# The output projection of two recurrences computed by itself and added to x in DRAM

## The chip, the cores and the metric

One core of a Trainium2 chip. The metric is the device time of one execution in microseconds: 3542.82 us, the median of three runs (3540.81 to 3544.31). The engines are named as in the profile: PE is TensorE, DVE is VectorE, ACT is ScalarE, POOL is GpSimd, and SP issues DMAs.

## The reference, cut to what matters

Two blocks of a network run one after the other on x (512 tokens by 1024 channels, float32). The first has two layers, each of them

```python
x = x + 0.5 * swiglu(rms_norm(x, ffn_norm[l, 0]), ...)
p = rms_norm(x, mix_norm[l]) @ w_in[l]
pa, pb, pc = split_cols(p, GROUP_SPLITS)
ya = dsa_attention(pa, ...)           # 512 channels
yb, v_first = rwkv7_time_mix(pb, ...) # 256 channels
yc = gated_deltanet(pc, ...)          # 256 channels
x = x + jnp.concatenate([ya, yb, yc], axis=-1) @ w_out[l]
x = x + 0.5 * swiglu(rms_norm(x, ffn_norm[l, 1]), ...)
```

The change touches the line with `w_out` in both layers. The 1024 input channels of that product are eight groups of 128: groups 0 to 3 come from the attention, 4 and 5 from the first recurrence (RWKV), 6 and 7 from the second (gated delta net). The second block is not touched.

## The kernel before

Everything is kept with channels on the 128 partitions and the 512 tokens along the free dimension, so x is eight tiles of 128x512. A float32 product is made of three matmuls (`mm3`): both operands are split into a high and a low part (`split`, `slab`), and high by high, high by low and low by high are accumulated in one PSUM bank. Weights come in slabs of 128x1024: a DMA issued by SP into one of three raw buffers, a cast on ACT and a subtraction on DVE into one of two pairs of high and low buffers.

The class `Mix` is one layer's middle part. It stores x to a DRAM tile `xd`, since the eight `x` buffers serve the attention meanwhile, computes the projections, two halves of each recurrence and the attention for four token tiles, and ends with the output projection by `down`.

The order of instructions on each engine isn't the order of the code. A planner sorts it when the kernel is built: among the instructions that can run, by its own estimate of times, the one with the smallest priority number comes first, and buffers and banks are handed out in that order. `stream(tag, level)` sets both the priority (a higher level is taken later) and the pool of buffers. The recurrences run at levels 0 and 1, the attention (`att`) at level 1, the weights and `down` at level 2, and the split of the recurrences' outputs into `yh` and `yl` at level 5. Once sorted, each engine runs its list strictly in order.

PSUM has eight banks in four pairs: `pj` (projections), `c` and `a` (the two halves of a recurrence) and `x` (the attention). For the last two token tiles the attention takes its transposed probabilities `pT` from the `pj` pair (`att(2, "x", "pj")` and `att(3, "x", "pj")`), four transposes to a bank, then a copy to SBUF by DVE or ACT in turn, and then the matmuls into `o`. In `att`, eight heads go in two groups of four; for tile 3 each group has four `pT` banks.

`down` works on half of the output channels at a time: four banks, one for each 128 channels, take all eight input groups, and then DVE adds each bank to x. For `Mix` the first half uses the pairs `c` and `a`, the second `pj` and `x`. Input groups are taken in the order 4, 5, 6, 7, 0, 1, 2, 3, two to a slab. So the first half's matmuls for the recurrences can run while the attention still works, and everything of the second half waits for `pj` and `x`. Before it x is loaded back from `xd` into eight fresh buffers. The following feed-forward part begins with the first four tiles of the new x.

Of the kernel before, what the change touches and what calls it, by code (L numbers as in the profile page):

```python
# [14 lines left out]
ALU = mybir.AluOpType  # L15
# [81 lines left out]
class Net:  # L97
# [3 lines left out]
    def __init__(self, ctx, tc, cst):  # L101
        self.ctx, self.tc, self.nc = ctx, tc, tc.nc
        nc = self.nc
        self.xp = ctx.enter_context(tc.tile_pool(name="xp", bufs=1))
        self.sm = ctx.enter_context(tc.tile_pool(name="sm", bufs=2))
        self.fp = ctx.enter_context(tc.tile_pool(name="fp", bufs=1))
        self.wraw = ctx.enter_context(tc.tile_pool(name="wraw", bufs=3))
        self.whi = ctx.enter_context(tc.tile_pool(name="whi", bufs=2))
        self.wlo = ctx.enter_context(tc.tile_pool(name="wlo", bufs=2))
        self.ps = ctx.enter_context(tc.tile_pool(name="ps", bufs=1, space=bass.MemoryType.PSUM))  # L110
        self.dr = ctx.enter_context(tc.tile_pool(name="dr", bufs=1, space=bass.MemoryType.DRAM))
        self.cst = self.xp.tile([128, _CN], F32, name="cst")
        self.reset = self.xp.tile([128, T], BF16, name="reset")
        nc.gpsimd.memset(self.reset, 1.0)
        nc.gpsimd.memset(self.reset[:, 0:T:64], 0.0)
        self.uid = 0
        self.tags = ["cag"[i % 3] for i in range(33)] + ["c", "a"] * 5 + ["g"]
        self.tag = "w"
        self.base = 0
        self.next = {}  # L120
# [207 lines left out]
class Mix:  # L328
# [3 lines left out]
    def __init__(self, net, l, x, par, w_in, lup, v_down, v_up, w_out, vfirst):  # L332
        self.n, self.tc, self.nc = net, net.tc, net.nc
        self.l, self.x, self.par, self.w_in, self.vfirst = l, x, par, w_in, vfirst
        nc, n = self.nc, net
        self.sm = net.sm
        (self.xh, self.xl, self.r), self.rc = net.split_x(x, self.p("mix_norm"))
        xd = n.dr.tile([128, KD, T], F32, name=f"xd{l}")
        for k in range(KD):
            nc.sync.dma_start(out=xd[:, k], in_=x[k])  # L340
        self.lp = net.xp.tile([128, 256], F32, tag="lp", name="lp")
        nc.scalar.dma_start(out=self.lp, in_=lup)
        if l:
            self.v_down, self.v_up = v_down, v_up
        self.kr = []
        self.y, self.yh, self.yl = [None] * 8, [None] * 8, [None] * 8
        chain = lambda tag="c", level=0: n.stream(tag, level)

        def go(part, tag="c", level=0):

            with n.stream(tag, level):
                next(part, None)

        r0, r1, g0, g1, at = self.rwkv(0), self.rwkv(1), self.gdn(0), self.gdn(1), self.att_in()
        self.misc()
        with chain("x", 1):
            self.index_in()
        with chain("c", 0):
            self.rwkv_in()
            self.kr.append(self.rwkv_kr(0))  # L360
        with chain("a", 0):
            self.kr.append(self.rwkv_kr(1))
        with chain("x", 1):
            for t in range(1, 4):
                self.index(t)
        go(r0, "c", 0)
        go(r1, "a", 0)
        go(at, "g", 1)
        with chain("c", 0):
            self.gdn_in()  # L370
        go(g0, "c", 0)
        go(r0, "c", 0)
        go(at, "g", 1)
        go(g1, "a", 0)
        go(r1, "a", 0)
        go(g0, "c", 1)
        go(g1, "a", 0)
        go(g0, "c", 0)
        with chain("g", 1):
            self.att(0, "x", "x")  # L380
            self.att(1, "x", "x")
        go(g1, "a", 0)
        with chain("g", 1):
            self.att(2, "x", "pj")
        with chain("g", 1):
            self.att(3, "x", "pj")
            self.att_out()
        with n.stream("c", 5):
            for i in (4, 5, 6, 7):
                self.yh[i], self.yl[i] = n.f("yh", F32R), n.f("yl", F32R)  # L390
                n.split(self.y[i], self.yh[i], self.yl[i])
        x[:] = [n.f("x", tag="x") for _ in range(KD)]
        with n.stream("w", 2):
            for k in range(KD):
                nc.sync.dma_start(out=x[k], in_=xd[:, k])
            net.down(x, self.yh, self.yl, w_out, [4, 5, 6, 7, 0, 1, 2, 3], 1.0,
                     (("c", "c", "a", "a"), ("pj", "pj", "x", "x")))

    def p(self, name, j=None):
        o, n = _PO[name]  # L400
# [1189 lines left out]
```

## Time and profile before

| | |
|---|---|
| median of three runs | 3542.82 us |
| the profiled execution's own time | 3542.9 us |
| its span | 3541.1 us |
| PE busy | 3414.4 us, 96% of the span |
| DVE busy | 2010.9 us, 57% |
| ACT busy | 1274.9 us, 36% |
| POOL busy | 84.7 us, 2% |
| mean granted PE clock | 0.965 |
| traffic with HBM | 100 GB/s over the span |

The span is what the profiler sees between the first and the last instruction; 1.8 us of the execution lie outside it. A share of busy time is a mean over very different stretches: the feed-forward parts have PE busy without a gap, the two `Mix` parts end in a stretch of small, dependent steps. Layer 0's output projection lies between 748 and 834 us of the span, layer 1's ends at 2023 us. In the timeline a line shows start, length, engine, line of the code, operation, output and inputs, and how many instructions are merged; a matmul's shown length is longer than the distance to the next one, because matmuls overlap.

### The profile page before, as it was taken

How to read it: one execution, taken by the hardware profiler on the slowest of the kernel's cores; microseconds unless marked ns; L12 is line 12 of the kernel's file. 1: busy time of each engine (PE TensorE's matmuls, PEld its weight loads, DVE VectorE, ACT ScalarE, POOL GpSimd, SP SyncE). 2: the span in 40 equal slices, each digit the busy share in tenths (PEclk: the TensorE clock that was granted, in tenths of full speed). 3: DMA queues.
4: the chain of work that ended last, by engine and by line, in shares of the span. 5: the costliest groups of instructions: out<-in, count | busy, mean ns of one | idle time of the engine just before them, and what ended most of it. 6: DMA issues, size and time to landing. Idle time of an engine off the chain costs nothing.

```text
span 3541.1 us, 44468 instructions
## 1 busy us (share of the span) xinstructions
PE 3414.4 (96%) x17314; PEld 2801.3 (79%) x17314; DVE 2010.9 (57%) x4364; ACT 1274.9 (36%) x2060; POOL 84.7 (2%) x168
## 2 busy tenths in 40 slices
PE   8999999889999999999998899999999999989999
PEld 7888778668888888887877688888777888778887
DVE  5555688765555555559978555535785332473332
ACT  4332544453332233335344433324563222232321
POOL 0000010000000000001100000000000000000000
PEclk9999999789999999999978999999999999989999
DMA  5346321103335434552210233432202333223332
GB/s 164 119 140 210 112 66 50 30 16 115 123 122 190 152 119 122 192 156 65 52 49 14 84 115 124 131 110 79 78 7 83 96 100 97 69 78 99 97 95 95
DMA packets 329955, 355.73 MB, mean 100 GB/s; under 512 B 41192, under 2 KB 249480, under 8 KB 329616
## 3 DMA queue, kind: packets, MB, share of 16 engines
q1 hardware_dynamic: 328576, 351.03, 32.5%
q8 instruction: 136, 2.23, 0.3%
q10 hardware_dynamic: 1168, 1.85, 0.2%
q14 instruction: 75, 0.61, 0.1%
HBM read 338.68 MB, written 14.16 MB: 100 GB/s over the span
## 4 chain that ended last, share of the span: by engine, by line
PE 89%; DVE 7%; ACT 2%; issue 1%; DMA 1%; POOL 0%; SPq 0%; DVEq 0%; ACTq 0%; POOLq 0%
PE pg L168 13%; PE pg L170 13%; PE pg L169 13%; PE pd L168 8%; PE pd L169 8%; PE pd L170 8%; PE pf L169 2%; PE pf L170 2%; PE pf L168 2%; PE lv L691 2%; PE G L904 1%; PE pt L430 1%; PE pt L431 1%; PE pt L429 1%; DVE wlo L162 1%
## 5 line engine op out<-in xcount | busy, mean ns | idle before, releaser
L162 DVE TENSOR_TENSOR wlo<-wraw,whi 128x1024 fp32r<-128x1024 f32 (+2 forms) x504 | 609.3, 1209 | 958.8 <-ACT whi L161 958.1
L161 ACT CAST whi<-wraw 128x1024 fp32r<-128x1024 f32 (+2 forms) x504 | 524.8, 1042 | 1283.6 <-PE pd L169 505.4
L168 PE MATMUL pg<-xh,whi 128*128 128x512 f32 x2112 | 825.5, 391 | 14.1 <-ACT whi L161 10.6
L170 PE MATMUL pg<-xh,wlo 128*128 128x512 f32 x2112 | 824.0, 390 | 0.0
L169 PE MATMUL pg<-xl,whi 128*128 128x512 f32 x2112 | 823.9, 390 | 0.0
L168 PEld LDWEIGHTS pg<-xh,whi 128*128 128x128 f32 x2112 | 398.1, 189 | 97.0 <-ACT whi L161 10.6
L169 PEld LDWEIGHTS pg<-xl,whi 128*128 128x128 f32 x2112 | 397.9, 188 | 83.1 <-DVE xl L273 0.6
L170 PEld LDWEIGHTS pg<-xh,wlo 128*128 128x128 f32 x2112 | 397.6, 188 | 83.5 <-DVE wlo L162 0.8
L168 PE MATMUL pd<-h,whi 128*128 128x512 f32 x1056 | 410.9, 389 | 0.0
L170 PE MATMUL pd<-h,wlo 128*128 128x512 f32 x1056 | 410.9, 389 | 0.0
L169 PE MATMUL pd<-h,whi 128*128 128x512 f32 x1056 | 410.8, 389 | 0.0
L1106 DVE CUSTOM_DVE_ANT_0 araw<-araw,act 128x512 f32<-128x512 f32 x224 | 148.9, 688 | 145.9 <-DMA araw<-in_ada_w_dram 140.6
L169 PEld LDWEIGHTS pd<-h,whi 128*128 128x128 f32 x1056 | 198.2, 188 | 41.3
L170 PEld LDWEIGHTS pd<-h,wlo 128*128 128x128 f32 x1056 | 198.2, 188 | 41.2
L168 PEld LDWEIGHTS pd<-h,whi 128*128 128x128 f32 x1056 | 198.2, 188 | 40.9
L168 PE MATMUL pf<-xh,whi 128*128 128x512 f32 (+4 forms) x424 | 167.0, 395 | 0.9 <-ACT xh L272 0.9
L169 PE MATMUL pf<-xl,whi 128*128 128x512 f32 (+4 forms) x424 | 167.3, 395 | 0.4 <-DVE xl L273 0.4
L170 PE MATMUL pf<-xh,wlo 128*128 128x512 f32 (+4 forms) x424 | 166.7, 393 | 0.0
L294 ACT ACTIVATE t<-t 128x512 f32<-128x512 f32 x88 | 55.6, 632 | 252.4 <-DVE t L293 250.6
L174 DVE TENSOR_TENSOR h<-t,h 128x512 fp32r<-128x512 f32 x132 | 90.8, 690 | 65.0 <-ACT h L173 64.7
L173 ACT CAST h<-t 128x512 fp32r<-128x512 f32 x132 | 81.8, 620 | 123.6 <-DVE t L296 76.7
L169 PEld LDWEIGHTS pf<-xl,whi 128*128 128x128 f32 (+2 forms) x424 | 79.1, 187 | 17.9 <-DVE xl L273 2.5
(494 smaller groups left out, 4692.8 us busy)
## 6 DMA issues: line engine op xcount, KB each, us to landing
wraw<-in_ffn_w_dram SPq DMA_DIRECT2D x132, 512.0 KB, 3.7
araw<-in_ada_w_dram SPq DMA_DIRECT2D x112, 512.0 KB, 3.5
wraw<-in_ffn_w_gate_dram SPq DMA_DIRECT2D x88, 512.0 KB, 3.8
wraw<-in_ffn_w_up_dram SPq DMA_DIRECT2D x88, 512.0 KB, 4.5
wraw<-in_ffn_w_down_dram SPq DMA_DIRECT2D x88, 512.0 KB, 3.6
wraw<-in_w_in_dram SPq DMA_DIRECT2D x69, 512.0 KB, 3.8
wraw<-in_w_out_dram SPq DMA_DIRECT2D x16, 512.0 KB, 3.5
xd<-x SPq DMA_DIRECT2D x24, 256.0 KB, 4.1
```

The costliest lines, as they stand in the source:

```text
L161: nc.scalar.copy(out=hi[:, :k * n], in_=raw[:, :k * n])
L162: nc.vector.tensor_sub(out=lo[:, :k * n], in0=raw[:, :k * n], in1=hi[:, :k * n].bitcast(F32))
L168: mm(out, lhsT=wh, rhs=xh, start=start, stop=False)
L169: mm(out, lhsT=wh, rhs=xl, start=False, stop=False)
L170: mm(out, lhsT=wl, rhs=xh, start=False, stop=stop)
L173: self.nc.scalar.copy(out=hi, in_=src)
L174: self.nc.vector.tensor_sub(out=lo, in0=src, in1=hi.bitcast(F32))
L294: nc.scalar.activation(out=t1, in_=t1, func=AF.Silu)
L429: mm(o, lhsT=self.xh[kk][:, ts], rhs=wh[:, k], start=s0, stop=False)
L430: mm(o, lhsT=self.xh[kk][:, ts], rhs=wl[:, k], start=False, stop=False)
L691: nc.tensor.matmul(b[:, i * 128:(i + 1) * 128], lhsT=lhs[th][:, i], rhs=rhs(th, i) if callable(rhs) else rhs[th][:, i], start=(i == 0), st ...
L1106: nc.vector.tensor_tensor_reduce(out=r[:, i], in0=r[:, i], in1=act, scale=1.0, scalar=0.0, op0=ALU.mult, op1=ALU.add, accum_out=acc[:, j + ...
```

## The change

The recurrences' four input groups are taken out of `down`. A new loop handles them two at a time: for each of the eight output tiles it takes one bank of the `pj` pair, makes six matmuls (two groups, three each), copies the bank to an SBUF buffer `po` by ACT, and has POOL issue a DMA that adds `po` to the tile of x in DRAM. There are 16 such units in a layer, and `po` has the four buffers of the tag `w`. `down` keeps the attention's four groups. The loop, the loads of x and `down` are all at level 3.

```diff
                 n.split(self.y[i], self.yh[i], self.yl[i])
+
+        with n.stream("w", 3):
+            for i in (4, 6):
+                for half in range(2):
+                    wh, wl = n.slab(w_out[i * 128:(i + 2) * 128, half * 512:(half + 1) * 512].rearrange("(k p) n -> p k n", p=128), 2, 512)
+                    for d in range(4):
+                        b, po = n.bank("po"), n.f("po")
+                        for k in range(2):
+                            c = slice(d * 128, (d + 1) * 128)
+                            n.mm3(b, wh[:, k, c], wl[:, k, c], self.yh[i + k], self.yl[i + k], k == 0, k == 1)
+                        nc.scalar.copy(out=po, in_=b)
+                        nc.gpsimd.dma_start(out=xd[:, half * 4 + d], in_=po, accum_op=ALU.add)
         x[:] = [n.f("x", tag="x") for _ in range(KD)]
-        with n.stream("w", 2):
+        with n.stream("w", 3):
             for k in range(KD):
                 nc.sync.dma_start(out=x[k], in_=xd[:, k])
-            net.down(x, self.yh, self.yl, w_out, [4, 5, 6, 7, 0, 1, 2, 3], 1.0,
-                     (("c", "c", "a", "a"), ("pj", "pj", "x", "x")))
+            net.down(x, self.yh, self.yl, w_out, [0, 1, 2, 3], 1.0, (("c", "c", "a", "a"), ("pj", "pj", "x", "x")))
```

## Rows read from the trace of the kernel before

**Rows 1.** The profile page's chain of waits: share of the span by engine.

```profile
PE 89%; DVE 7%; ACT 2%; issue 1%; DMA 1%; POOL 0%; SPq 0%; DVEq 0%; ACTq 0%; POOLq 0%
```

**Rows 2.** Busy time by stretch, layer 0: us, busy time (instructions), PE clock, DMA.

```profile
748.00:764.00 16.00, 15.45 (x102) 11.35 (x102) 8.99 (x36) 8.32 (x21) 0.00 (x0) 1.00 0.00 1
764.00:777.00 13.00, 10.46 (x48) 8.51 (x49) 10.46 (x33) 6.97 (x16) 1.26 (x1) 0.87 0.01 1
777.00:784.00 7.00, 6.20 (x38) 4.00 (x36) 3.90 (x13) 6.98 (x18) 0.00 (x0) 1.00 0.00 0
784.00:790.00 6.00, 3.73 (x13) 1.69 (x12) 4.20 (x13) 3.72 (x8) 0.00 (x0) 0.78 0.54 174
790.00:802.00 12.00, 8.57 (x35) 4.43 (x34) 2.92 (x10) 5.04 (x13) 0.00 (x0) 0.54 0.35 102
802.00:834.00 32.00, 32.00 (x143) 26.48 (x142) 16.31 (x24) 12.11 (x18) 0.00 (x0) 1.00 0.34 106
```

**Rows 3.** Timeline of PE: output projection and the next part's first matmul, both layers.

```profile
748.13 0.40 PE L168 MATMUL pd<-yh,whi 128*128 128x512 f32 x1
...
779.03 0.40 PE L170 MATMUL pd<-yh,wlo 128*128 128x512 f32 x1
...
801.58 0.73 PE L168 MATMUL pd<-yh,whi 128*128 128x512 f32 x2 [1.07 <-ACT yh L173]
...
834.35 0.39 PE L168 MATMUL pg<-xh,whi 128*128 128x512 f32 x1
...
1990.50 0.73 PE L168 MATMUL pd<-yh,whi 128*128 128x512 f32 x2 [1.07 <-ACT yh L173]
...
2023.27 0.39 PE L168 MATMUL pg<-xh,whi 128*128 128x512 f32 x1
```

**Rows 4.** Timeline of PE, layer 0: transposes and output matmuls of the last attention tile.

```profile
776.50 0.38 PE L436 MATMUL pT<-cst,p 128*128 128x128 f32 x2
...
781.14 1.08 PE L628 MATMUL o<-pT,v 128*64 128x256 f32 x8
782.15 0.98 PE L436 MATMUL pT<-cst,p 128*128 128x128 f32 x7
...
789.82 1.05 PE L436 MATMUL pT<-cst,p 128*128 128x128 f32 x4
...
794.94 1.97 PE L628 MATMUL o<-pT,v 128*64 128x256 f32 x8
796.85 1.75 PE L436 MATMUL pT<-cst,p 128*128 128x128 f32 x7
798.53 1.98 PE L628 MATMUL o<-pT,v 128*64 128x256 f32 x8
```

**Rows 5.** Timeline of ACT, layer 0: copies out of the `pj` banks.

```profile
783.61 0.58 ACT L626 COPY pT<-pT 128x512 f32<-128x512 f32 x1
...
798.64 0.58 ACT L626 COPY pT<-pT 128x512 f32<-128x512 f32 x1 [4.16 <-PE pT L436]
```

**Rows 6.** Timeline of DVE, layer 0: last split of a recurrence, first addition to x.

```profile
776.14 0.68 DVE L174 TENSOR_TENSOR yl<-yo,yh 128x512 fp32r<-128x512 f32 x1
...
809.35 1.41 DVE L324 SCALAR_TENSOR_TENSOR x<-pd,x 128x512 f32<-128x512 f32 x2
```

**Rows 7.** Timeline of POOL, layer 0, 760 to 812 us: everything that it runs there.

```profile
764.78 1.26 POOL L472 TENSOR_TENSOR qtm<-qtm,ropet 128x512 f32<-128x512 f32 x1 [23.14 <-DVE rst L203]
```

**Rows 8.** DMA issues of 256 KB: count, KB each, median us to landing.

```profile
xd<-x SPq DMA_DIRECT2D x24, 256.0 KB, 4.1
x<-xd SPq DMA_DIRECT2D x24, 256.0 KB, 4.3
...
out_dram<-x SPq DMA_DIRECT2D x8, 256.0 KB, 2.0
```

**Rows 9.** Timeline of SP's DMA queue, layer 0, 785 to 812 us.

```profile
796.10 4.80 SPq L395 DMA_DIRECT2D x<-xd  x8
809.46 0.38 SPq L160 DMA_DIRECT2D wraw<-in_w_out_dram  x1
```

## The prediction

> **What bounds the kernel now.** I read the chain of waits first: PE carries 89% of it [rows 1], so time is won where PE waits, or where work sits behind PE's last wait and could have run before it. Then I cut the end of layer 0's `Mix` into stretches [rows 2]. The reader is to see three things there. From 802 to 834 us PE is busy for all 32 of 32 us at the full clock of 2.4 GHz (1.00). From 784 to 802 it is busy for 3.73 + 8.57 of 18 us, and the granted clock is 0.78 and then 0.54, so part of that busy time runs at the 1.2 GHz level. And DVE and ACT aren't full either, with 7.12 and 8.76 us in those 18: the last attention tile is a chain of short steps that hand over to each other.
>
> Then the timeline says what the full stretch is. The output projection starts at 748.13, does the first half of the recurrences' share by 779.03, stands still, and starts again at 801.58 when the attention's last split arrives; the next part's first matmul is at 834.35 [rows 3]. Half 0 of the recurrences is 4 groups x 4 tiles x 3 = 48 matmuls, already beside the attention. Behind 801.58 lie 48 (half 0, attention) + 48 (half 1, recurrences) + 48 (half 1, attention) = 144 matmuls, and 834.35 - 801.58 = 32.77 us, 0.2276 us each. Layer 1 is the same to a hundredth: 2023.27 - 1990.50 = 32.77 [rows 3]. Those 48 recurrent matmuls of half 1, 10.9 us in each layer, are what the change can move. It removes no matmul.
>
> **The change part by part.** All sums are made against the profiled execution's own 3542.9 us (span 3541.1 and 1.8 around it), which is within 0.1 us of the median of 3542.82.
>
> (a) What leaves the full stretch: 48 x 0.2276 = 10.9 us a layer, if all 16 units (six matmuls, 1.37 us each) find room before the attention ends.
>
> (b) What doesn't find room. Units need a bank of `pj`, and there are two. Groups 4 and 5 are ready by 748; the first eight units take the stretch 748 to 777, where today's 48 early matmuls already sit. Groups 6 and 7 need the last split, which ends at 776.14 + 0.68 = 776.8 [rows 6]. But from 776.50 the transposes of the last tile's first head group hold both `pj` banks, until the copy that ends at 784.2; the second group takes them at 789.82 and holds them until 799.2 [rows 4, 5]. So the free windows for eight units are 784.2 to 789.8, 5.6 us or four units, and the wait before 801.58, one unit. I take R = 3 left over, 3 x 1.37 = 4.1 us; the ends are R = 0 (another bank taken a little later costs the attention nothing, since its fourth head is what gates the copy) and R = 8, 10.9 us, where the move gains nothing.
>
> (c) The attention's own end. In the second head group the chain's PE pieces run at the lower clock: 1.97, 1.75 and 1.98 us against 1.08, 0.98 and 1.08 for the same instruction counts in the first group [rows 4], 2.6 us in all. What PE did before differs: in the first group projection matmuls ran between them, in the second PE idled for over a third of 784 to 790 [rows 2]. The new units fall in just that gap, so the clock should fall later or not at all. I take half, -1.3 us, because from 790 on the banks are taken and PE is thin again; ends 0 and -2.6.
>
> The Trainium skill, "TensorE: Matmul & The Clock Gate", Part 1, says that the clock follows how busy the PE has recently been; the rows agree, 0.54 after the idle gap. By that rule alone the whole 2.6 would come back, and the sum below would be 2.6 us lower.
>
> (d) ACT. 16 copies of a bank at 0.58 us [rows 5] are 9.3 us a layer. ACT has room, 9.2 us free from 784 to 802 [rows 2], but its list is in order: behind a copy wait the exponentials, the casts and every second copy of `pT`, and for those wait PE and DVE. Some five copies fall beside the second group's chain; a step that comes up behind one waits half of 0.58 on average, at some five handovers: +1.5 us. Ends 0 and, five whole copies, 2.9.
>
> (e) POOL. Its one instruction in the stretch is the rotation of the last tile's queries at 764.78, 1.26 us [rows 7], and that is on the attention's chain. POOL's queue now holds DMA issues, each waiting for ACT's copy. What is queued behind a waiting issue is this rotation, and for it wait the query's transposes. The trace has no DMA issued by POOL. At most one issue stands ahead: 0 to 1.3 us (as long as the one POOL row there), and since the attention goes first in the planner's order I take 0.3, near the lower end.
>
> (f) The accumulating DMA. No row shows one. Bounds from plain 256 KB transfers: 2.0 us, the output stores, and 8.4, a load of 4.3 and a store of 4.1 after each other, since it reads the tile and writes it back [rows 8]. I take 5, next to a plain `xd` store with some reading added. With four `po` buffers, the fifth copy must wait for the first landing; at 1.37 us a unit that is 5.5 us later, of which the copy is 0.6, so up to about 5 us cost nothing: 0. At 8.4 the ACT list waits 3.5 us in each round of four: in two rounds of a layer 7 us, the other end.
>
> The Trainium skill, "DMA: Bandwidth & Descriptors", Anatomy of one DMA, fits 2.0 us + bytes / 436e3 for DMAs issued from GpSimd; the estimate for 256 KB is 2.6 us, a plain copy, and no run here shows it. By it the term stays 0.
>
> (g) Loads of x. They now wait for the last addition of their tile. SP issued them at 796.10, and DVE first used x at 809.35 [rows 6, 9]. Tiles 0 to 3 have their last unit before or near the attention's end, so at about 800 + 5 + 4.3 they are there by 809.3, and the first use comes later by R units: 0. Tiles 4 to 7 get their last addition near 806; 806 + 0.6 + 5 + 4.3 = 816, and their use comes 10.9 + 6.8 us after the last unit, near 823. SP stands at these loads until about 811.6, against 809.46 for the next slab's issue before [rows 9], 2 us that two finished slabs (5.5 us of matmuls each) and the loaded raw ones hide. Without that cover it costs those 2 us.
>
> (h) Slabs: eight before and after, the same casts. Level 3 in place of 2: nothing else of a lower level is left to run, 0.
>
> Sum for a layer: -10.9 + 4.1 - 1.3 + 1.5 + 0.3 = -6.3; two layers -12.6. 3542.9 - 12.6 = 3530.3, so 3530. With the likelier parts of the ends (R from 1 to 5, ACT from 0.5 to 2.9) the forecast's own range is 3520 to 3536.
>
> **The rivals.**
>
> *The gain is given back within the attention.* If R is 5 or more, or ACT's copies and the two banks hold the chain up by 3 us, what is left is -10.9 + 6.8 + 1.5 + 0.3 - 0 = -2.3 a layer, and 3538. For it: `pj` is exactly the pair that the chain needs, from 776.50 on almost without a break, and a unit that has begun holds its bank for 1.37 us and a copy. A unit for groups 6 and 7 can even begin on group 6 and then hold its bank until 776.8 for group 7. Against it: today's early matmuls are woven into the first head group just as closely, and from its first transposes to its last copy that group takes 7.7 us (776.50 to 784.2), the second 9.4 (789.82 to 799.2).
>
> *It gets slower: the `po` buffers run out.* One mechanism: the planner spaces copies for a landing that the chip doesn't keep, and ACT, in order, stops at the fifth copy with the exponentials behind it. The place is the stretch 764 to 802, the price (L + 0.6 - 5.5) for every four units, in two rounds of a layer. It decides from where it outweighs 6.3: L of 8 us. At L = 12 it is 14.2 a layer, net +7.9, two layers +15.8: 3559. For it: read, add and write in one DMA has no row. Against it: all plain 256 KB rows lie at 4.3 or below [rows 8], and the DMA engines are idle there but for 784 to 802 (shares 0.54 and 0.35) [rows 2].
>
> *All of it hides and the clock stays up.* R = 0, the clock's 2.6 in full, and 1 us of the wait before 801.58: -10.9 - 2.6 + 0.3 - 1 = -14.2 a layer, 3514.5. It asks for free banks that [rows 4, 5] don't show.
>
> A case in which the change doesn't do what it says, all units behind the attention (R = 8), is the first rival at its end: -10.9 + 10.9, so 3543.
>
> **How the numbers follow.** About 0.2% of the time, 7 us, is what a measurement of this kernel can tell from no change. Forecast 0.49; given back 0.25; slower 0.18; all hidden 0.08. The forecast counts as faster but for its upper end; all hidden does too: 0.56. The first rival is within 7 us: with that upper end 0.27. Slower: 0.17. The range to hold 8 times in 10 leaves out most of "all hidden" and the worse half of the slower one: 3515 to 3552. The likeliest case's own range, 3520 to 3536, stands beside it.
>
> **What would show it.** Right: the next part's first matmul comes 21.9 us plus about three units after the attention's last split, not 32.8; four or so units lie between 784 and 790, and the clock there is 1.00; the landing of the new DMAs is near 5 us. Wrong: `pT` transposes that wait for a copy of `po`; ACT idle in front of a `po` copy, released by a DMA; DVE waiting at its addition for a load of x; and an attention that ends later than 801.58 by more than 2 us.

## The result and the profile after

The changed kernel takes 3585.98 us, the median of four runs (3570.13 to 3596.03), against 3541.82 for the kernel before beside it (3539.62 to 3544.31). That is 44 us slower, where 3530 and a range to 3552 were forecast. The ratio on record is 1.0112, with a 95% interval of 1.0078 to 1.0146; it isn't the quotient of the two medians, which is 1.0125 and lies inside the interval. The profiled execution took 3587.43 us, its span is 3585.6.

PE's share of the chain of waits fell from 89% [rows 1] to 86%, and DVE, DMA and "issue" (time in which an engine waits for nothing that the profile shows) have a point more each:

```profile
PE 86%; DVE 8%; issue 2%; DMA 2%; ACT 2%; POOL 0%; SPq 0%; DVEq 0%; ACTq 0%; POOLq 0%
```

The same stretches of layer 0 as in [rows 2], with the same columns:

```profile
748.00:764.00 16.00, 13.94 (x80) 9.38 (x80) 7.97 (x34) 7.69 (x18) 0.00 (x0) 0.83 0.01 2
764.00:777.00 13.00, 7.45 (x23) 4.66 (x23) 9.66 (x29) 6.28 (x20) 1.26 (x1) 0.50 0.00 0
777.00:784.00 7.00, 3.62 (x11) 1.75 (x11) 3.94 (x16) 5.64 (x11) 0.00 (x0) 0.50 0.00 0
784.00:790.00 6.00, 6.00 (x26) 3.38 (x26) 1.55 (x4) 0.84 (x2) 0.00 (x0) 0.55 0.01 3
790.00:802.00 12.00, 7.57 (x30) 3.75 (x29) 3.68 (x15) 6.41 (x13) 0.00 (x0) 0.76 0.00 0
802.00:834.00 32.00, 29.76 (x123) 22.37 (x122) 6.42 (x9) 15.12 (x26) 13.08 (x15) 0.93 0.85 155
```

From 764 to 784 PE has 34 instructions where it had 86, and the granted clock is 0.50, the 1.2 GHz level, where it was 0.87 and 1.00. The stretch behind 802 is no longer full: 29.76 of 32 us, at 0.93.

The timeline of PE says why (code behind the new loop stands 11 lines further down, so line 447 is 436 of before and 639 is 628):

```profile
741.37 0.66 PE L729 MATMUL bR<-GA,WU 128*64 128x128 f32 x8
...
799.08 1.98 PE L639 MATMUL o<-pT,v 128*64 128x256 f32 x8
800.99 1.76 PE L447 MATMUL pT<-cst,p 128*128 128x128 f32 x7
802.67 1.40 PE L639 MATMUL o<-pT,v 128*64 128x256 f32 x8
804.00 0.50 PE L168 MATMUL po<-yh,whi 128*128 128x512 f32 x1
...
819.43 0.50 PE L168 MATMUL po<-yh,whi 128*128 128x512 f32 x1 [2.19 <-ACT po L402]
...
820.32 0.63 PE L168 MATMUL po<-yh,whi 128*128 128x512 f32 x1
820.75 0.63 PE L169 MATMUL po<-yl,whi 128*128 128x512 f32 x1
...
852.56 0.39 PE L168 MATMUL pg<-xh,whi 128*128 128x512 f32 x1
...
1950.21 0.76 PE L729 MATMUL bR<-GA,WU 128*64 128x128 f32 x8
...
2011.18 1.40 PE L639 MATMUL o<-pT,v 128*64 128x256 f32 x8
2012.50 0.50 PE L168 MATMUL po<-yh,whi 128*128 128x512 f32 x1
...
2061.46 0.39 PE L168 MATMUL pg<-xh,whi 128*128 128x512 f32 x1
```

The first matmul of a unit starts at 804.00, right behind the attention's last product, and in layer 1 at 2012.50. In neither layer did one of the sixteen units run beside the attention. The 48 matmuls that did run there before, from 748.13 on [rows 3], were moved behind it as well.

Two stretches can be compared across kernels, since the instructions that bound them are always there. The first goes from the last product `bR` of a recurrence (before the change acts) to the end of the last matmul into `o`: the attention's end. The second goes from there to the next part's first `pg`: the output projection. In the kernel before they begin with these rows, and end by the rows at 798.53 [rows 4], 834.35 and 2023.27 [rows 3]:

```profile
742.50 0.66 PE L718 MATMUL bR<-GA,WU 128*64 128x128 f32 x8
...
1931.12 0.76 PE L718 MATMUL bR<-GA,WU 128*64 128x128 f32 x8
...
1987.89 1.53 PE L628 MATMUL o<-pT,v 128*64 128x256 f32 x8
```

Before, that is 58.0 + 33.8 us in layer 0 and 58.3 + 33.9 in layer 1; after, 62.7 + 48.5 and 62.4 + 48.9. A layer lost 4 to 5 us in the attention's end and about 15 in the projection, 38.4 us in both layers of the 44.5 between the spans. Of these 15 us, 10.9 are 48 more matmuls at 0.2276 us, and some 4 are waits of the kind at 819.43, after which the clock dips too (from 820.32 on the matmuls are 0.43 us apart).

The projection's waits begin at the new DMAs. The lines of the tile `po`: the copies and issues (ns, minimum, median, maximum), what ACT's copies waited for (us, times), and the landing:

```profile
L402 ACT COPY po<-po x32: 572/587/588, 805.7 to 2043.4; 128x512 f32<-128x512 f32 x32
L403 POOL DMA_DIRECT2D xd<-po x32: 853/862/1056, 806.6 to 2044.3; - x32
...
  DMA xd<-po: 21.9, 16
...
DMA to landing us min/median/max: 4.2/7.3/9.7
```

A copy needs one of four buffers; the buffer is free when its DMA has landed, 7.3 us after the issue, and a unit takes 1.37 us. So from the fifth unit on ACT waits for landings, 16 times and 21.9 us over both layers; the two `pj` banks stay full meanwhile, and PE stands.

### The profile page after: what moved, and what is told of

Read it like the earlier page. It is cut to its first block, busy times and chain, and to the rows that moved or that the text cites. A ratio compares the mean times of both kernels' runs of the same rounds, so it can differ in the third digit from the quotient of the medians.

```text
span 3585.6 us, 44606 instructions
## 1 busy us (share of the span) xinstructions
PE 3434.3 (96%) x17314; PEld 2807.0 (78%) x17314; DVE 2012.3 (56%) x4364; ACT 1294.1 (36%) x2092; POOL 111.8 (3%) x200
## 3 DMA queue, kind: packets, MB, share of 16 engines
q0 software_dynamic: 4608, 8.39, 1.5%
HBM read 338.68 MB, written 22.54 MB: 101 GB/s over the span
## 4 chain that ended last, share of the span: by engine, by line
PE 86%; DVE 8%; issue 2%; DMA 2%; ACT 2%; POOL 0%; SPq 0%; DVEq 0%; ACTq 0%; POOLq 0%
PE pg L168 13%; PE pg L169 13%; PE pg L170 13%; PE pd L168 7%; PE pd L169 7%; PE pd L170 7%; PE pf L169 2%; PE pf L170 2%; PE pf L168 2%; PE lv L702 2%; PE G L915 1%; PE pt L441 1%; PE pt L442 1%; PE pt L440 1%; PE o L1379 1%
```

## The experiments

Each edit is made in the changed kernel, but for that of e1_order, which is made in the kernel before. The table gives the median, the ratio to the kernel before on the same chip with its 95% interval, and for each layer the two stretches (attention's end + projection) of the profiled run, read from the same rows as above. The kernel before took 3554.01 us beside e1 to e4, 3546.83 beside e5 to e8 and 3545.40 beside e9 to e11.

| run | us | ratio | layer 0 | layer 1 | both, against before |
|---|---|---|---|---|---|
| before | 3541.82 | | 58.0 + 33.8 | 58.3 + 33.9 | |
| after | 3585.98 | 1.0112 (1.0078 to 1.0146) | 62.7 + 48.5 | 62.4 + 48.9 | +38.4 |
| e1_order | 3578.45 | 1.0081 (1.0050 to 1.0112) | 60.0 + 44.7 | 62.4 + 44.7 | +27.8 |
| e2_po17 | 3586.62 | 1.0096 (1.0063 to 1.0129) | 59.6 + 44.7 | 62.4 + 44.4 | +27.0 |
| e3_level | 3585.47 | 1.0104 (1.0067 to 1.0141) | 81.3 + 27.6 | 84.1 + 25.9 | +34.9 |
| e4_banks | 3524.91 | 0.9929 (0.9903 to 0.9956) | 58.0 + 25.2 | 57.5 + 25.9 | -17.3 |
| e5_again | 3593.53 | 1.0129 (1.0094 to 1.0164) | 60.0 + 48.0 | 62.4 + 49.2 | +35.5 |
| e6_banks17 | 3530.22 | 0.9952 (0.9923 to 0.9981) | 56.8 + 25.0 | 57.7 + 25.0 | -19.5 |
| e7_code | 3566.45 | 1.0056 (1.0031 to 1.0081) | 77.3 + 23.0 | 79.9 + 23.0 | +19.1 |
| e8_plain | 3576.66 | 1.0098 (1.0065 to 1.0131) | 60.0 + 44.9 | 60.9 + 44.4 | +26.3 |
| e9_half1 | 3530.87 | 0.9956 (0.9936 to 0.9976) | 55.3 + 25.9 | 55.4 + 25.9 | -21.6 |
| e10_ptx | 3559.81 | 1.0046 (1.0032 to 1.0061) | 74.2 + 25.7 | 69.3 + 24.9 | +10.0 |
| e11_banks2 | 3533.87 | 0.9971 (0.9947 to 0.9996) | 59.6 + 26.1 | 58.2 + 25.9 | -14.2 |

Runs of one kernel spread over some 40 us here, the kernel before included (3521.94 to 3566.42 in the first group). At least a part of that comes from code which no edit touches: before the change acts, the last `bR` of layer 0 is at 741.4 in the first profile of the changed kernel and at 762.7 in its second, e5_again. One stretch of each, the first profile above, the second below (columns as in [rows 2]):

```profile
500.00:748.00 248.00, 224.38 (x1637) 183.34 (x1636) 208.19 (x667) 99.95 (x214) 21.27 (x39) 0.90 0.16 39
```

```profile
500.00:748.00 248.00, 227.60 (x1443) 182.45 (x1442) 194.32 (x626) 91.12 (x194) 18.90 (x34) 0.80 0.16 40
```

The same kernel got a clock of 0.90 once and 0.80 the other time, and 194 fewer matmuls in it. So a few us are read from the two stretches and not from the medians; for every run the last column lies within 12 us of the difference of its medians. The stretches have noise of their own, and each stands on one profile: the changed kernel's two profiles differ by 2.7 us in the attention's end of layer 0 (62.7 and 60.0), and e4_banks and e11_banks2, one kernel as well, by 1.6. The kernel before has one profile only.

**What keeps the units out.** Theory 1: among the requests for one pair of banks, the planner hands the banks out in the order in which the code makes them, and not, as the section on the kernel before says, in the order of the priorities. `po` asks for `pj` after the last tile's `pT`, so it gets none before the attention's last transposes. Rivals: the level is too low; the loss is not the order at all but the DMAs.

The level alone:

```diff
-        with n.stream("w", 3):
+        with n.stream("w", 0.5):
             for i in (4, 6):
```

> The changed kernel with the loop of the units at level 0.5 in place of 3, so that it goes ahead of the attention in priority; the place in the code is unchanged. Theory 1 (banks of one pair are handed out in the order in which the code asks for them, so no unit gets a pj bank before the attention's last pT): nearly nothing changes, the first po matmul stays behind the attention's last pT transposes, 3580 to 3592. Rival (the level is too low): units fall beside the attention from 748 us on, and the time comes to 3525 to 3545.

It took 3585.47 us. In PE's timeline the units stand behind the last transposes and now ahead of the last products:

```profile
808.94 1.62 PE L447 MATMUL pT<-cst,p 128*128 128x128 f32 x7
810.62 0.50 PE L168 MATMUL po<-yh,whi 128*128 128x512 f32 x1
...
831.68 0.65 PE L639 MATMUL o<-pT,v 128*64 128x256 f32 x2
...
838.11 0.40 PE L168 MATMUL pd<-yh,whi 128*128 128x512 f32 x1
```

With a number smaller than the attention's they went ahead of the last products, whose wait makes the attention's end 81.3 and 84.1 us, and yet not of a single `pT`. The priority isn't what held them.

The place in the code alone:

```diff
-        with chain("g", 1):
-            self.att(3, "x", "pj")
-            self.att_out()
         with n.stream("c", 5):
             for i in (4, 5, 6, 7):
...
                         nc.gpsimd.dma_start(out=xd[:, half * 4 + d], in_=po, accum_op=ALU.add)
+        with chain("g", 1):
+            self.att(3, "x", "pj")
+            self.att_out()
```

> The changed kernel with the split of the recurrences' outputs and the units' loop written ahead of the last token tile's attention in place of behind it; same pj banks, same level. Theory 1 (banks of a pair go out in the order of the code): all 96 unit matmuls now come ahead of the last tile's pT transposes and none behind the attention, so 96 x 0.2276 = 21.9 us and no more lie between the last split and the next part; but the last tile's transposes wait for the units' banks, 21.9 us of units less the PE time that is idle there (about 12 us): the attention ends some 10 us later than before, in all 3540 +- 10. Rival (the place in the code does not matter): as the changed kernel, 3580 to 3590.

All but the last two of the 96 unit matmuls now start ahead of the last tile's transposes, none lies behind the attention, and the projection is 23.0 us (96 x 0.2276, and 1.1 for the last split). That part of theory 1 holds. The time was expected at 3540 and is 3566.45: the attention's end grew by 19 and 22 us, nearly all of the units' 21.9, instead of 10. The chain has to wait for the banks until the whole block is done, and most of the time that PE is idle in the chain comes after the block and stays unused. And the block takes longer than its matmuls:

```profile
789.14 0.50 PE L621 MATMUL s<-kh,qs 128*128 128x512 f32 x1
789.48 0.40 PE L622 MATMUL s<-kl,qs 128*128 128x512 f32 x1
...
796.66 0.80 PE L168 MATMUL po<-yh,whi 128*128 128x512 f32 x1 [4.51 <-ACT po L399]
797.25 0.63 PE L169 MATMUL po<-yl,whi 128*128 128x512 f32 x1
...
814.95 0.61 PE L447 MATMUL pT<-cst,p 128*128 128x128 f32 x4
```

The lines left out are the units': between 789.48 and 814.95 PE runs nothing else. But of these 25 us it stands for 6.0, waiting for copies of `po`. The longest wait is the one shown: on ACT's list that copy comes behind the exponentials and casts of the first head group. After it, 14 matmuls are 0.43 us apart in place of 0.23, some 2.8 us more. These 8.8 us are about as much as layer 0 missed the expectation by; layer 1 has the same wait of 4.51 us.

The pair alone, in two ways. First the units take other banks:

```diff
-                        b, po = n.bank("po"), n.f("po")
+                        b, po = n.bank("po", "ccaa"[d]), n.f("po")
```

> The changed kernel with one edit: the units take their banks from the pairs c and a, which the recurrences have left, in place of pj. Theory 1: units come from 748 us on; 12 of the 96 unit matmuls are left behind the attention, and with the 96 of down 108 x 0.2276 = 24.6 us lie between the last split and the next part, against 32.8 before: up to 8.2 us a layer, 3526 if the attention ends where it did. If the copies, the four po buffers (each held until a DMA lands 7 us later) and the units on PE hold the attention up by more than that: 3543 to 3560. If the order of the banks is not the cause, it stays at 3580 to 3590.

It took 3524.91 us, 0.9929 of before; once more on another chip 3533.87, 0.9971 (0.9947 to 0.9996):

> The kernel with unit banks from c and a (four po buffers) once more, beside half 1 alone on one chip: tail 67.4 us a layer, 8.6 less than before, so 17 us less: a ratio of 0.995, and 0.993 as the first time is within its noise.

The tail, from the last product `bY` of a recurrence to the next part's first `pg`, is 69.5 and 67.8 us in that second run, where 67.4 was expected. The timeline of PE in layer 0 of the first:

```profile
745.46 0.39 PE L168 MATMUL po<-yh,whi 128*128 128x512 f32 x1
...
794.25 1.08 PE L639 MATMUL o<-pT,v 128*64 128x256 f32 x8
...
796.75 1.08 PE L639 MATMUL o<-pT,v 128*64 128x256 f32 x8
797.77 0.50 PE L168 MATMUL po<-yh,whi 128*128 128x512 f32 x1
...
800.62 0.39 PE L168 MATMUL pd<-yh,whi 128*128 128x512 f32 x1
...
823.06 0.39 PE L168 MATMUL pg<-xh,whi 128*128 128x512 f32 x1
```

Units start at 745.46, the last group's products take 1.08 us in place of 1.97 and 1.98 (the granted clock is 1.00, the 2.4 GHz level, over the last 20 us of the attention's end, where it was 0.67), and 25.2 us lie behind the attention. A second way: the attention takes its `pT` elsewhere.

```diff
-            self.att(2, "x", "pj")
+            self.att(2, "x", "x")
-            self.att(3, "x", "pj")
+            self.att(3, "x", "x")
```

> The changed kernel with the last two token tiles' pT in the pair x in place of pj: the units keep pj to themselves. Theory 1 (what keeps the units out is that they ask for pj after pT in the code): units come from 748 us on, and 92 matmuls or 20.9 us lie behind the attention. But o holds one bank of x all along, so s and pT share the other, and 14 transposes with their copies stand one behind the other in place of overlapping: some 0.8 us each, 11 us; tail 42 + 11 + 1 + 21 = 75 us, the time of before within 8 us. Rival (something else in the order holds the units back, as their level): units stay behind the attention and the tail is over 95 us, 3590 or more.

The units, left as they were, come from 750.16 on, and the projection is 25.7 and 24.9 us. The attention's end is 11 to 16 us longer, as its transposes share a pair with `s` and `o`; expected 11, and at 3559.81 against 3545.40 it is 14 us slower than before, outside the 8 us expected. The cause of the order is shown by these four edits: another level brings no unit ahead of a `pT`, another place in the code or another pair does. The planner's rule itself is read off from its orders.

**What the order costs by itself.** In the kernel before, with no units and no DMAs:

```diff
-            net.down(x, self.yh, self.yl, w_out, [4, 5, 6, 7, 0, 1, 2, 3], 1.0,
+            net.down(x, self.yh, self.yl, w_out, [0, 1, 2, 3, 4, 5, 6, 7], 1.0,
```

> The kernel before with one edit: down takes the input groups in the order 0 to 7, so that all 192 matmuls of a layer's output projection come after the attention's last split, with no po bank, no copy, no accumulating DMA. Theory 1 (the change is slow because all sixteen units lie behind the attention, so that the 48 matmuls that ran beside it left its end empty): 48 x 0.2276 = 10.9 us a layer more behind the attention, and about 4.7 us a layer more in the attention's end, whose clock falls to 0.50: 2 x 15.6 = 31 us, 3573; the stretch 764 to 784 shows 0.50 as the changed kernel does. Rival A (the attention's loss there is not from the missing matmuls but from the copies or the DMAs on the engines' lists): 2 x 10.9 = 22 us, 3564, and the attention's end stays within 1 us of 801.6. Rival B (the whole loss is the accumulating DMA and its buffers): no more than 7 us slower than before.

The projection is 44.7 us, 10.9 more than before, and the attention's end 2.0 and 4.1 us longer, with nothing on ACT or POOL that wasn't there before. The windows of layer 0 (its attention ends at 823.0):

```profile
784.00:790.00 6.00, 3.81 (x16) 2.60 (x14) 3.61 (x9) 1.20 (x2) 1.26 (x1) 0.50 0.00 0
790.00:802.00 12.00, 5.93 (x16) 3.12 (x15) 8.76 (x33) 10.14 (x27) 0.00 (x0) 0.64 0.00 0
802.00:823.00 21.00, 16.04 (x67) 8.04 (x66) 6.54 (x20) 8.43 (x16) 0.00 (x0) 0.70 0.10 29
```

PE has little work here, and the granted clock is 0.50 to 0.70. The median, 24 us above that of before, can't choose between 31 and 22; the stretches give 27.8, and the attention's part of them, 6.1, is more than rival A allows, though layer 0's 2.0 alone is within the noise of a stretch. e5_again, the changed kernel's second profile, has the same attention's end as this run to 0.02 us in both layers (60.02 and 62.36 against 60.01 and 62.35), so the copies and DMAs add nothing there. So 27.8 of the 38.4 us come without any unit in the kernel: most of the loss has nothing to do with the units' own work. That the missing matmuls lengthen the attention's end by way of the clock is read from the traces: the clock granted over the attention's end is 0.86 and 0.85 before, 0.77 and 0.75 in e1_order, and 1.00 and 0.97 in e4_banks. No run changes the clock alone.

**What the DMAs cost.** More buffers, and then a plain DMA in place of the accumulating one:

```diff
-                        b, po = n.bank("po"), n.f("po")
+                        b, po = n.bank("po"), n.f("po", tag="a")
```

> The changed kernel with po taken from the seventeen buffers of the tag a in place of the four of w; order of PE as in the changed kernel. If the stalls among the units are the four po buffers that wait for the accumulating DMA to land (ACT idle 21.9 us in front of po copies): 4.9 us a layer come back, 3586 - 10 = 3576, and PE runs the 192 matmuls of a layer in 43.7 to 44.5 us. If the stalls only move to the loads of x, which wait for the same DMAs: 3583 or above, and DVE's first addition to x waits for a load.

```diff
-                        nc.gpsimd.dma_start(out=xd[:, half * 4 + d], in_=po, accum_op=ALU.add)
+                        nc.gpsimd.dma_start(out=xd[:, half * 4 + d], in_=po)
```

> The changed kernel with plain DMAs in place of accumulating ones: it leaves out the addition of the recurrences' part to x. If the accumulating DMA's own slowness (7.3 us to land, against 4.1 for a plain store of 256 KB in the kernel before) is what empties the four buffers: the landing falls to about 4 us, the 4.9 us of stalls a layer go, 3576. If landing is as late with plain DMAs (the descriptors' issue on POOL or the queue is what is slow): 6 us or more to land and 3583 to 3590.

The changed kernel itself was run beside the second of these:

> The changed kernel itself once more, on the chip of the other runs of this group, so that they can be compared with it: its tail is the same instructions, so from the last recurrence matmul bY to the next part's first matmul 96 us in both layers as before, and 3575 to 3595.

In e2_po17 and e8_plain the projection falls from between 48.0 and 49.2 us to between 44.4 and 44.9, which is its length in e1_order, which has no DMA. So the waits are the four buffers, 4 us a layer, and the accumulating DMA's landing is what empties them. The lines of `po` with seventeen buffers:

```profile
L403 POOL DMA_DIRECT2D xd<-po x32: 853/865/1115, 821.3 to 2048.4; - x32
...
DMA to landing us min/median/max: 4.2/9.1/11.6
```

and with plain DMAs and four:

```profile
L403 POOL DMA_DIRECT2D xd<-po x32: 539/539/710, 805.7 to 2033.1; - x32
...
  DMA xd<-po: 3.0, 4
...
DMA to landing us min/median/max: 2.3/4.0/7.0
```

No copy waits for a DMA with the seventeen buffers (that line is gone), though the landing is later still; that more of them are in flight at once is the likely reason, but wasn't tested. The medians are too rough for 8 us in two layers: e2_po17 doesn't show them (3586.62, where 3576 was expected), and e8_plain is 17 us below e5_again. The size stands on the stretches.

**Versions that beat both kernels.** Both edits together:

> The changed kernel with both edits: unit banks from the pairs c and a, and po from the seventeen buffers of a. In the run with c and a alone 12 of 96 unit matmuls were left behind the attention and ACT waited 3.3 us for landings. If the buffers no longer cost anything there: within 3 us of that run, 3522 to 3528, since the planner leaves 14 unit matmuls in place of 12 behind the attention. If copies held back by landings still delay the attention's list on ACT: up to 7 us less, 3518.

It is 0.9952 of before; its two stretches are together 0.8 to 3.9 us a layer shorter than those of e4_banks and e11_banks2. That hints at a small cost of the four buffers even there, but these two, one kernel, are up to 2.5 us a layer apart themselves. And half of the change: only output half 1 goes through `po`, four units of twelve matmuls.

```diff
-            for i in (4, 6):
-                for half in range(2):
+            for half in (1,):
+                pb = [n.bank("po", "ccaa"[d]) for d in range(4)]
+                for i in (4, 6):
...
-            net.down(x, self.yh, self.yl, w_out, [0, 1, 2, 3], 1.0,
+            net.down(x, self.yh, self.yl, w_out, ([4, 5, 6, 7, 0, 1, 2, 3], [0, 1, 2, 3]), 1.0,
```

> Half of the change: for output half 0 the recurrences stay in down (groups 4 to 7 first, in the banks c and a, as in the kernel before); only for half 1 they are computed apart, four units of twelve matmuls in the banks c and a ahead of half 0's, so four copies and four accumulating DMAs a layer in place of sixteen. By the planner's order 18 recurrent matmuls are left behind the attention, with half 0 and half 1 of the attention 114 x 0.2276 = 25.9 us: from the last bY to the next part 42.0 + 1.1 + 25.9 = 69 us, 7 us a layer less than before, 3529. If the sixteen copies and DMAs cost the attention anything in the run with banks c and a, this one is faster than its 67.5 us tail; if they cost nothing, it is slower by the 6 matmuls, 1.4 us a layer.

It is 0.9956 of before, and its two stretches are the shortest of all, some 81.2 us together in either layer. Its tail is 64.8 us, where 69 was expected. With four copies and four issues in place of sixteen the attention's end is 55.3 and 55.4 us, 2.2 to 4.3 us shorter than with sixteen in e4_banks and e11_banks2. Its interleaving on PE differs too, so the gain isn't shown to be that of the copies and issues. By the medians, the three faster versions can't be told apart.

## Why the prediction was wrong

- **(b) is the step that failed.** It said that units need a bank of `pj`, and filled the windows in which the trace shows none of them occupied, "the free windows for eight units are 784.2 to 789.8". A bank that stands empty in the trace was not on offer here: it went to whoever asked earlier in the code, and the units asked last (e3_level, e7_code, e4_banks). The step also let the first eight units inherit the place of "today's 48 early matmuls"; those had it because they asked for `c` and `a`. The prediction's end for this term, R = 8 and 3543, still left eight units beside the attention. With all sixteen behind it the term is +21.9, and (a) and (b) together +10.9 a layer where -6.8 was forecast. With some 4.4 in the attention's end and some 4 of waits for buffers, these are the 19.2 a layer by which the two stretches grew.
- **(a)** The size was right: 48 x 0.2276 = 10.9, against the 10.87 by which the projection of e1_order is longer than before (44.71 less 33.84). It came with the other sign.
- **(c)** Forecast -1.3, between 0 and -2.6. Measured +4.7 and +4.1 in the attention's end (+2.0 and +4.1 in e5_again), and +2.0 and +4.1 with no unit in the kernel. One of its readings is off as well: the third "1.08" is no row of the first head group. The products at 783.53 take 1.36 us in the trace, since half of them wait for the copy that ends at 784.2; with that row the difference is 2.3 us, not 2.6. The same reasoning (PE without work beside the chain gets the lower clock) was applied to work coming in, while the work went out. Where units do come in, e4_banks, the products of layer 0 are back at 1.08 us. The Trainium skill, "TensorE: Matmul & The Clock Gate", Part 1, which the prediction quoted, says that the clock follows how busy the PE has recently been; the traces agree with it in both directions: 0.50 from 764 to 784 us after the change, where PE has 34 instructions in place of 86, and 0.97 to 1.00 over the attention's end of e4_banks.
- **(d), (e)** Not put to the test by the change, since no copy or issue fell beside the attention. In e4_banks and e11_banks2 they did: attention's end 58.0 and 57.5 us, and 59.6 and 58.2, against 58.0 and 58.3. So there (c), (d) and (e) sum to between -0.8 and +1.6, where +0.5 was forecast. The three terms can't be told apart in it. The last queries' rotation on POOL didn't wait for an issue in e4_banks.
- **(f)** 5 us was taken for the landing, with 8.4 as the end and 7 us a layer as its price. It is 7.3 in the median, up to 9.7, and cost about 4 us a layer: the right mechanism at another place. It held up the units themselves, not the exponentials. The Trainium skill, "DMA: Bandwidth & Descriptors", Anatomy of one DMA, gave an estimate of 2.6 us for 256 KB; the plain DMA from POOL landed in 4.0 and the accumulating one in 7.3, and the measurement decides.
- **(g), (h)** Held. SP stood 19.7 us at the eight loads of x in layer 0, but PE runs from the last unit to 852.56 without a gap.
- **The rivals.** The slower one named the buffers, which are some 8 of the 44 us, and set its threshold on a price inside the attention. Its counterpart for the order, that all units fall behind the attention, stood in the text, but as a move that "gains nothing" instead of a loss. The argument that all plain 256 KB rows lie at 4.3 or below doesn't hold for the whole trace, which has loads with medians of 4.8, 5.5 and 5.7 us. There was a hint of the order in the kernel before: half 1 of `down` asks for `pj` after `pT` and gets to work only at the end. It was no more than a hint, since half 1 also comes behind half 0 in the code.

About 6 us of the 44.5 between the two spans lie outside both stretches, in code that is the same in both kernels. With shifts of up to 23 us between profiles before the change even acts, this remainder wasn't traced to anything.

## What to carry to other kernels

When work is moved to other buffers or banks, ask who else asks for them and in which order the code does so; a bank that looks free in the trace may already be promised to work that asked earlier in the code. Work that fills the gaps of a chain of small steps does two jobs, its own and keeping PE's clock up, so taking it out costs more than its own length (13.9 us a layer for 10.9 in e1_order). And of work that has to pass through DRAM, try to send less: four sums in place of sixteen gave the shortest tail here, though its median can't be told from that of the versions with sixteen.

## What the runs showed of the hardware

- An accumulating 256 KB DMA into DRAM, issued by POOL, lands in 7.3 us in the median with four source buffers and 9.1 with seventeen (after, e2_po17), against 4.0 for a plain one from the same four (e8_plain). Where the same 32 are spread out beside the attention the median is 6.3 (e4_banks) or 4.6 (e10_ptx). Its issue takes POOL 0.86 us against 0.54.
- The profile counts the traffic of an accumulation once: the queue of these DMAs shows 8.39 MB for 32 transfers of 256 KB, and HBM reads stay at 338.68 MB as before.
- The same kernel's clock differs from run to run in a stretch of small steps, 0.90 and 0.80 between 500 and 748 us (after, e5_again). The last `bR` of layer 0 is 21 us later in the second, and the whole span 14 us longer.
